# A conditioning matmul read in whole rows beside the first MLP, and an output projection that begins before the last DeltaNet head ends

## The chip, the cores and the metric

The kernel runs on one core of a Trainium2 chip. The metric is the device time of one launch in microseconds (us). Five engines matter: PE (TensorE, the matmuls; PEld is its weight load), DVE (VectorE), ACT (ScalarE), POOL (GpSimd) and SP (SyncE), whose queue here issues nearly all loads. Each engine, and each queue of transfers, works strictly in the order in which its instructions stand.

## The reference

One denoising step of a two-layer backbone over 640 tokens (128 context tokens and 512 latent tokens, width D = 1024). Layer 0 mixes tokens by softmax attention, layer 1 by gated DeltaNet with 8 heads; each layer ends in a squared-ReLU MLP of width 4096. Before each mixer and each MLP the activations are normalised and modulated by vectors that come from a conditioning vector:

```python
def modulation(cond, w_mod, b_mod):
    m = jax.nn.silu(cond) @ w_mod + b_mod
    return jnp.split(m[..., None, :], N_MOD, axis=-1)

def trunk_layer(x, mods, gain1, gain2, w1, w2, mixer):
    shift1, scale1, gate1, shift2, scale2, gate2 = mods
    mix, aux = mixer(rms_norm(x, gain1) * (1 + scale1) + shift1)
    x = x + gate1 * mix
    h = rms_norm(x, gain2) * (1 + scale2) + shift2
    x = x + gate2 * (jnp.square(jax.nn.relu(h @ w1)) @ w2)
    return x, aux
```

The DeltaNet mixer ends, for every head, in a gated norm, and then in the output projection over all heads:

```python
    o = rms_norm(o, norm_gain) * jax.nn.silu(z.reshape(B, T, DN_HEADS, DN_DV).astype(jnp.float32))
    out = o.reshape(B, T, DN_VAL).astype(h.dtype) @ w_out
```

## The kernel before, in words

Activations lie transposed: 8 tiles of 128 features by 640 tokens, handled in two halves of 320 tokens. A matrix product is made of column tiles of 128 output features. For one column tile and one half, each of 8 feature tiles takes three matmuls (`mm3`: high part by high part, high by low, low by high), 24 matmuls of 128x128 by 320 columns into one PSUM bank. Weights are loaded by SP into one of 3 `raw` buffers; ACT writes the high part and DVE (or POOL, where `eng` says so) the low part. The parts lie in `wpair` (6 buffers, 3 pairs; names `w`, `xin`, `y`) or in `wext` (10 buffers, names `wx`). `prefetch` fills `wpair` with the first three column tiles of the next product.

Python generators issue the program; a scheduler then sets the order on each engine and waits are added where a buffer or a value is not there yet. `pinned` runs the first MLP (128 steps of one column tile and half each) beside side work (`beside`), one side step for so many MLP steps. The side work is first the modulation of layer 1, slab 0: 1024 rows of `w_mod` by 2048 columns, as 8 feature rows k of four quarters q of 512 columns. Quarter q is a matmul with only 32 weight columns, put at column 32 q of the array; it writes rows 32 q to 32 q + 31 of one bank. A quarter in float32 shows as two MATMUL records. `modulate_pieces` loads a quarter (256 KB) into one of three `rawp` buffers and issues one quarter in each side step. After it `presplit` splits the DeltaNet's weights through `rawp` and `wpair` and writes them to DRAM.

In `delta` the heads pass through a pipeline of rounds (`weave` mixes the steps). `dn_out` ends a head: squares on ACT, a reciprocal root in small DVE operations, a multiply of the head's output (POOL for heads 0 to 6, DVE for head 7), five transposes on PE, the gate on DVE and a split into high and low. Heads 0 to 4 go to DRAM (`outd`) and are loaded and split again by `load_act` after the last round. Then the pool of `delta` closes, `mlp1` opens, `x` is loaded back (`reload`, from `xs`) and `dense` makes the output projection: three prefetched column tiles, then the other five as one group, whose low parts POOL makes. `residual` adds each half tile to `x` and, by `norm_acc`, its squares to a sum.

Of the kernel before, what the change touches and what calls it, by code (L numbers as in the profile page):

```python
# [8 lines left out]
F32 = mybir.dt.float32  # L9
# [6 lines left out]
P = 128  # L16
D = 1024
FT = D // P
# [3 lines left out]
HALF = T // 2  # L22
NBLK = T // P
HEADS = 8
# [9 lines left out]
HALVES = ((0, HALF), (HALF, T))  # L34
# [3 lines left out]
GROUP = 5  # L38
# [3 lines left out]
DIRECT = 5  # L42
# [35 lines left out]
def weave(*parts):  # L78
    live = [[0, n, i, g] for i, (g, n) in enumerate(parts)]
    while live:  # L80
        live.sort(key=lambda e: ((e[0] + 1) / e[1], e[2]))
        e = live[0]
        try:
            next(e[3])
            e[0] += 1
        except StopIteration:
            live.pop(0)
# [5 lines left out]
def pinned(tc, main, n, side, m):  # L93
    nc = tc.nc
    last = {}
    why = mybir.DependencyInfo(mybir.DependencyClass.NoSync, mybir.DependencyReason.DATA)
    traced = lambda i: nc.cur_bb.bb.instructions[i:]
    at = len(traced(0))
    done = step = 0
    for _ in main:  # L100
        step += 1
        for i in traced(at):
            if i.engine in PINNED:
                last[i.engine] = i.name
        at = len(traced(0))
        while done * n < step * m and next(side, True) is None:
            done += 1
            for i in traced(at):
                if i.engine in last:
                    tc.add_manual_dep(i, last[i.engine], why, reason="paced")  # L110
            at = len(traced(0))
    drain(side)


def drain(g):
    for _ in g:
        pass


class Model:  # L120
# [332 lines left out]
    def piece(self):  # L453
        return self.scr("rawp", 3, [P, FT // 2, P])

    def modulate_pieces(self, l, slab):
        ps = self.ps("mod", 1)[:, :512]

        def load(n):
            k, q = divmod(n, 4)  # L460
            r = self.piece().rearrange("p k c -> p (k c)")
            c = slab * 2048 + q * 512
            self.nc.sync.dma_start(out=r, in_=self.a["w_mod"][l, k * P : (k + 1) * P, c : c + 512])
            return r

        raws = [load(n) for n in range(2)]
        for n in range(4 * FT):
            k, q = divmod(n, 4)
            if n + 2 < 4 * FT:
                raws.append(load(n + 2))  # L470
            self.nc.tensor.matmul(  # L471
                ps[32 * q : 32 * q + 32, :], self.cond[:, k, :], raws.pop(0),
                start=k == 0, stop=k == FT - 1, tile_position=(0, 32 * q),
            )
            yield
        yield from self.modulation(l, slab, ps, lambda: self.ps("mod", 1))

    def fetch_slots(self, src):
        out = []
# [295 lines left out]
    def psum(self, name):  # L775
        return self.tc.tile_pool(name=name, bufs=1, space=bass.MemoryType.PSUM)
# [204 lines left out]
    @staticmethod  # L981
    def b3(t):
        return t.rearrange("p (b i) -> p b i", b=NBLK)
# [251 lines left out]
    def dn_out(self, hd):  # L1235
        nc = self.nc
        st, b3 = self.st[hd], self.b3
        o = st["o"]
        sso = self.small("sso", [P, NBLK], 2)
        self.squares(self.main("a"), o, sso)  # L1240
        self.ts(sso, sso, 1.0 / P, ALU.mult, P * EPS * EPS, ALU.add)
        self.stt(sso, st["ssc"][:, 1, :], P * EPS, sso, ALU.mult, ALU.add)
        sso = self.rsqrt(sso)
        eng = nc.gpsimd if hd < HEADS - 1 else nc.vector
        self.tt(b3(o), b3(o), sso.unsqueeze(2).to_broadcast([P, NBLK, P]), ALU.mult, eng)
        ps = self.ps("big", 2, 1024)
        for s in self.blocks():
            self.tr(ps[:, s], o[:, s])
        out = self.main("a")
        self.stt(out, ps[:, :T], self.dg, st["z"], ALU.mult, ALU.mult)  # L1250
        if hd < DIRECT:
            nc.gpsimd.dma_start(out=self.outd[hd], in_=out)
        else:
            self.split_act(hd, out)
        del self.st[hd]
        yield

    def delta(self, h, first):
        nc, a = self.nc, self.a
        self.st, self.acts = {}, {}  # L1260
        self.outd = self.dp.tile([HEADS, P, T], F32, tag="outd", bufs=1, name="outd")
        self.lev = self.scr("lev", 1, [P, P])
        nc.sync.dma_start(out=self.lev, in_=a["lev"])
        self.levcols = self.scr("levc", 1, [P, sum(P // b for b in LEVELS[1:])])
        nc.sync.dma_start(out=self.levcols, in_=a["levcols"])
        NP = 64 + NBLK * NB
        self.pn = self.scr("pn", 1, [NP, BASE * BASE])
        self.pt = self.scr("ptri", 1, [NP, BASE * BASE])
        nc.vector.memset(self.pn, 0.0)
        nc.vector.memset(self.pt, 0.0)  # L1270
        nc.vector.memset(self.pt[:, :: BASE + 1], 1.0)
        done = []

        def gated(zs):
            for i in zs:
                yield from self.dn_z(h, i)
                if i < HEADS - 1:
                    yield from self.dn_out(i)
                done.append(i)

        def mods():
            for slab in (1, 2):
                yield from self.modulate(1, slab, self.fetch_mixed, self.dense_ps, True)

        wm = mods()
        for r in range(HEADS + 3):
            parts = []
            if 0 <= r - 3 < HEADS:
                parts.append((self.dn_scan(r - 3), 14))
            if 0 <= r - 2 < HEADS:  # L1290
                parts.append((self.dn_inverse(r - 2), 10))
            if 0 <= r - 1 < HEADS:
                parts.append((self.dn_decay(r - 1), 20))
            zs = ZROUNDS.get(r, ())
            if zs:
                parts.append((gated(zs), 20 * len(zs)))
            if r < HEADS:
                parts.append((self.dn_dense(h, r, first if r == 0 else None), 54))
            if r >= HEADS:
                parts.append((islice(wm, MODS[r - HEADS]), MODS[r - HEADS]))  # L1300
            weave(*parts)
        drain(wm)
        self.first = self.prefetch(a["dn_w_out"][0], 0, [f * P for f in range(FT)])
        for i in range(DIRECT):
            self.load_act(i)
        drain(self.dn_out(HEADS - 1))

    def load_act(self, hd):
        f = self.main("x")
        self.nc.sync.dma_start(out=f, in_=self.outd[hd])  # L1310
        self.split_act(hd, f)

# [6 lines left out]
    def run(self):  # L1319
        tc, nc, a = self.tc, self.nc, self.a  # L1320
        pool = lambda name: tc.tile_pool(name=name, bufs=1)
        psum = self.psum
        FC = [f * P for f in range(FT)]
        with psum("ps0") as self.pq:
# [3 lines left out]
            x = []  # L1328
# [7 lines left out]
            h = self.first_norm(x, gm)  # L1336
        with pool("attn") as self.ph:
            self.attention(h, x)
            first = self.prefetch(a["attn_w_out"][0], 0, FC)
        with pool("mlp0") as self.ph, psum("ps3") as self.pq:  # L1340
            self.extra = 3
            x = self.reload(self.xd)
            h = self.new_h()
            nxt = []

            def mid():
                nxt[:] = self.prefetch(a["mlp_w1"][0], 0, FC)
                self.mod_norm(x, 0, 1, h, 0)

            weave((self.modulate(0, 2, self.fetch_raw), 18),  # L1350
                  (self.dense(a["attn_w_out"][0], 0, FC, self.att, self.residual(x, 0, 2), first=first, last=GROUP, mid=mid), 16))
            self.mod_norm(x, 0, 1, h, 1)
            h2 = self.new_h()
            nxt2 = []

            def mid2():
                w = a["dn_w_in"][0]
                nxt2[:] = [self.pair(w, 0, kind * D) for kind in (1, 0, 2)]
                self.mod_norm(x, 1, 0, h2, 0)

            def beside():
                yield from self.modulate_pieces(1, 0)
                yield from self.presplit()

            pinned(tc, self.mlp(0, h, x, nxt, mid2), 128, beside(), 98)
            self.mod_norm(x, 1, 0, h2, 1)
            h = h2
            xd = self.spill(x, nc.scalar)
        with pool("delta") as self.ph, psum("ps4") as self.pq:
            self.extra = 0  # L1370
            self.delta(h, nxt2)
        with pool("mlp1") as self.ph, psum("ps5") as self.pq:
            self.extra = 4
            acts = [self.acts[i] for i in range(HEADS)]
            x = self.reload(xd)
            h = self.new_h()
            nxt3 = []

# [1 line left out]
                nxt3[:] = self.prefetch(a["mlp_w1"][1], 0, FC)  # L1380
                self.mod_norm(x, 1, 1, h, 0)

            drain(self.dense(a["dn_w_out"][0], 0, FC, acts, self.residual(x, 1, 2), first=self.first, last=GROUP, mid=mid3, eng=nc.gpsimd))
            self.mod_norm(x, 1, 1, h, 1)
            fn = a["final_norm"]
            gain = self.wp.tile([P, D], F32, tag="wpair", bufs=self.NW, name="fgain")
# [73 lines left out]
```

## Time and profile before

| | us |
|---|---|
| median of 3 runs (lowest, highest) | 1906.38 (1905.86, 1908.35) |
| the profiled execution's own time | 1908.76 |
| its span, first to last instruction | 1906.9 |
| PE busy in it | 1816.6 (95%) |
| PEld, DVE busy | 1660.6, 990.3 |
| ACT, POOL busy | 754.5, 311.9 |
| granted TensorE clock, mean | 0.982 |

The span is one core's; 1.9 us of the profiled time lie outside it. A busy share is a mean over stages, so a stage is read by what its engines wait for there. A granted clock of 1.00 is 2.4 GHz, 0.50 is 1.2 GHz.

### The profile page before, as it was taken

To read this page: it belongs to the slowest core of one execution; us is meant where nothing else is said; L and a number is where in the kernel's file an instruction comes from. 1 tells how busy PE (TensorE), PEld (TensorE's weight loads), DVE (VectorE), ACT (ScalarE), POOL (GpSimd) and SP (SyncE) were. 2 spreads that over 40 slices of the span, in tenths; PEclk is the share of its full clock that TensorE was granted. 3 is DMA by queue.
4 is the path that set the end of the run, shared out by engine and by line. 5 is a ranking of instruction groups with operands and counts; after the bars stand their busy time and mean duration, and the time that the engine had idled before them with its cause. 6 is when DMAs were issued, how large, how long until landed. Compare 5 with 4: busy or idle time off the path is not lost.

```text
span 1906.9 us, 31083 instructions
## 1 busy us (share of the span) xinstructions
PE 1816.6 (95%) x11981; PEld 1660.6 (87%) x11981; DVE 990.3 (52%) x2293; ACT 754.5 (40%) x1725; POOL 311.9 (16%) x405
## 2 busy tenths in 40 slices
PE   6999999999999999999899999999899999999997
PEld 2778877888889999999889989776699999999997
DVE  4646662733244555555778877653655334343332
ACT  2445552421133443434756655623433223131331
POOL 2344221400001111142212111110241000000012
PEclk8899999999999999999999999999899999999999
DMA  7651137323347787843434324563712222222211
GB/s 278 219 157 43 34 109 212 103 76 113 102 127 254 227 269 225 257 160 128 129 111 118 81 86 131 167 189 135 224 53 79 70 75 78 78 74 70 78 45 56
DMA packets 291370, 248.84 MB, mean 130 GB/s; under 512 B 45104, under 2 KB 247239, under 8 KB 291223
## 3 DMA queue, kind: packets, MB, share of 16 engines
q1 hardware_dynamic: 271376, 207.85, 36.4%
q0 software_dynamic: 9136, 32.18, 4.6%
q10 hardware_dynamic: 10710, 6.83, 1.2%
q8 instruction: 94, 1.54, 0.3%
q14 instruction: 54, 0.43, 0.1%
HBM read 199.00 MB, written 45.20 MB: 128 GB/s over the span
## 4 chain that ended last, share of the span: by engine, by line
PE 75%; DVE 15%; DMA 5%; issue 2%; ACT 1%; POOL 1%; SPq 1%; POOLq 0%; ACTq 0%; DVEq 0%
PE dense L173 33%; PE pd L173 29%; PE scan L173 3%; PE big L173 2%; DVE cv L166 2%; DVE ptmp L160 2%; PE mod L471 2%; PE pd L408 1%; PE mod L408 1%; DVE ptri L1083 1%; PE big L176 1%; DVE wide L160 1%; DVE a L160 1%; DMA ptmp<-gmd 1%; PE S L173 1%
## 5 line engine op out<-in xcount | busy, mean ns | idle before, releaser
L173 PE MATMUL pd<-h,w 128*128 128x320 f32 x2016 | 353.6, 320 | 10.7 <-ACT cv L163 6.3
L173 PE MATMUL dense<-a,wx 128*128 128x320 f32 x2238 | 340.9, 311 | 2.4 <-ACT wx L163 1.8
L173 PEld LDWEIGHTS dense<-a,wx 128*128 128x128 f32 x2238 | 332.5, 189 | 11.2 <-issue 4.2
L173 PEld LDWEIGHTS pd<-h,w 128*128 128x128 f32 x2016 | 300.6, 189 | 38.3 <-issue 21.8
L163 ACT ACTIVATE wx<-raw 128x1024 fp32r<-128x1024 f32 x132 | 139.6, 1058 | 369.8 <-PE dense L173 234.0
L173 PEld LDWEIGHTS dense<-h,wx 128*128 128x128 f32 x1776 | 261.5, 188 | 9.2 <-issue 9.2
L173 PE MATMUL dense<-h,wx 128*128 128x320 f32 x1776 | 266.9, 309 | 0.0
L160 DVE TENSOR_TENSOR wx<-raw,wx 128x1024 fp32r<-128x1024 f32 x127 | 159.2, 1256 | 163.9 <-ACT wx L163 142.3
L173 PE MATMUL pd<-a,wx 128*128 128x320 f32 x1284 | 195.1, 310 | 0.0
L173 PEld LDWEIGHTS pd<-a,wx 128*128 128x128 f32 x1284 | 189.7, 188 | 4.2 <-issue 1.7
L166 DVE SCALAR_TENSOR_TENSOR x<-dense,c,x 128x320 f32<-128x320 f32 (+2 forms) x152 | 61.9, 435 | 191.6 <-PE dense L173 191.5
L173 PE MATMUL pd<-h,wx 128*128 128x320 f32 x1008 | 152.7, 309 | 0.0
L173 PEld LDWEIGHTS pd<-h,wx 128*128 128x128 f32 x1008 | 148.7, 188 | 4.2 <-issue 3.4
L160 POOL TENSOR_TENSOR x<-x,half 128x320 f32<-128x320 f32 x48 | 54.6, 1137 | 515.7 <-ACT half L163 508.4
L163 ACT ACTIVATE a<-half 128x320 fp32r<-128x320 f32 x128 | 59.9, 471 | 115.0 <-DVE half L166 115.0
L925 POOL DMA_DIRECT2D wd<-w x58 | 31.1, 536 | 398.9 <-ACT w L163 355.1
L160 DVE TENSOR_TENSOR a<-half,a 128x320 fp32r<-128x320 f32 x128 | 62.7, 492 | 64.1 <-ACT a L163 64.0
L166 DVE SCALAR_TENSOR_TENSOR x<-pd,c,x 128x192 f32<-128x192 f32 (+2 forms) x88 | 35.9, 436 | 102.5 <-PE pd L173 102.4
L166 DVE SCALAR_TENSOR_TENSOR cv<-cv,c,cv 128x644 f32<-128x644 f32 x84 | 78.2, 931 | 20.0 <-ACT cv L163 18.9
L163 ACT ACTIVATE half<-x 128x320 f32<-128x320 f32 x56 | 26.1, 467 | 106.2 <-DVE x L166 106.1
L173 PE MATMUL big<-wide,a 128*128 128x128 f32 x480 | 63.4, 278 | 1.0 <-DMA wide<-td 0.9
L173 PEld LDWEIGHTS big<-wide,a 128*128 128x128 f32 x480 | 58.0, 191 | 5.8 <-ACT a L163 1.7
(286 smaller groups left out, 2528.4 us busy)
## 6 DMA issues: line engine op xcount, KB each, us to landing
raw<-in_mlp_w SPq DMA_DIRECT2D x128, 512.0 KB
wd<-w POOLq DMA_DIRECT2D x58, 512.0 KB, 4.7
w<-wd SPq DMA_DIRECT2D x58, 512.0 KB
raw<-in_w_mod SPq DMA_DIRECT2D x48, 512.0 KB
rawp<-in_dn_w_in SPq DMA_DIRECT2D x58, 256.0 KB
a<-in_w_mod SPq DMA_DIRECT2D x48, 256.0 KB
rawp<-in_w_mod SPq DMA_DIRECT2D x32, 256.0 KB
raw<-in_attn_w_in SPq DMA_DIRECT2D x12, 512.0 KB
```

The source lines that it names most:

```text
L160: (eng or self.nc.vector).tensor_tensor(out=out, in0=in0, in1=in1, op=op)
L163: self.nc.scalar.activation(out=out, in_=in_, func=func, **kw)
L166: self.nc.vector.scalar_tensor_tensor(out=out, in0=in0, scalar=s, in1=in1, op0=op0, op1=op1)
L173: self.nc.tensor.matmul(out, l, r, start=first, stop=last)
L176: self.nc.tensor.transpose(out, in_, self.ident[:n, :n])
L408: nc.tensor.matmul(ps[32 * q : 32 * q + 32, :], self.cond[:, k, :], views[q], start=k == 0, stop=k == FT - 1, tile_position=(0, 32 * q),)
L471: self.nc.tensor.matmul(ps[32 * q : 32 * q + 32, :], self.cond[:, k, :], raws.pop(0), start=k == 0, stop=k == FT - 1, tile_position=(0, 32 ...
L925: self.nc.gpsimd.dma_start(out=d[z], in_=pair[z].bitcast(F32).rearrange("p k c -> p (k c)"))
L1083: nc.vector.tensor_reduce(out=t[:, BASE * i : BASE * i + i], in_=o, axis=AX.X, op=ALU.add)
```

## The change

There are two parts. First, the modulation beside the first MLP goes through `modulate`, which the kernel already uses elsewhere, with a new `fetch_pairs`: each feature row k comes as two loads of 512 KB into the `wpair` buffers, one row ahead, and a side step issues all four quarters of a row. The modulation takes 9 side steps instead of 33, and the pacing number goes from 98 to 74.

Second, the output projection's three prefetched tiles, in both halves, begin inside `delta` (`out_begin`): six half tiles in six PSUM banks (two `dense`, two `scan`, two halves of one `big`), first heads 0 to 6 for all six, then head 7 for all six, then the six residual sums. `x` is reloaded before it. The squares of these three tiles are summed after the pool has closed, and the group of five follows as before. `load_act` now stands in the last round, behind head 7's gate projection, and loads into `h` buffers; the multiply of head 6 moves from POOL to DVE.

```diff
+    def fetch_pairs(self, src):
+        out = []
+        for i in range(2):
+            r = self.wp.tile([P, 2, 512], F32, tag="wpair", bufs=self.NW, name=self.nm("wm"))
+            self.nc.sync.dma_start(out=r, in_=src[:, i * 1024 : (i + 1) * 1024].rearrange("p (q c) -> p q c", q=2))
+            out += [r[:, 0, :], r[:, 1, :]]
+        return out
...
-        eng = nc.gpsimd if hd < HEADS - 1 else nc.vector
+        eng = nc.gpsimd if hd < HEADS - 2 else nc.vector
...
+            if i == HEADS - 1:
+                for j in range(DIRECT):
+                    self.load_act(j)
+                    yield
...
-        for i in range(DIRECT):
-            self.load_act(i)
         drain(self.dn_out(HEADS - 1))
 
+    def out_begin(self, x):
+        wide = self.ps("big", 2, 1024)
+        banks = [self.dense_ps() for _ in range(2)] + [self.ps("scan", 2) for _ in range(2)] + [wide[:, :512], wide[:, 512:]]
+        todo = [(o, half, banks.pop(0)[:, :HALF]) for o in range(len(self.first)) for half in range(2)]
+        for ks in (range(HEADS - 1), (HEADS - 1,)):
+            for o, half, ps in todo:
+                lo, hi = HALVES[half]
+                for k in ks:
+                    w, act = self.first[o], self.acts[k]
+                    self.mm3(ps, (w[0][:, k, :], w[1][:, k, :]), (act[0][:, lo:hi], act[1][:, lo:hi]),
+                             k == 0, k == HEADS - 1)
+        sink = self.residual(x, 1, 2, False)
+        for t in todo:
+            sink(*t)
...
-                yield from self.modulate_pieces(1, 0)
+                yield from self.modulate(1, 0, self.fetch_pairs, early=True)
                 yield from self.presplit()
 
-            pinned(tc, self.mlp(0, h, x, nxt, mid2), 128, beside(), 98)
+            pinned(tc, self.mlp(0, h, x, nxt, mid2), 128, beside(), 74)
...
             self.delta(h, nxt2)
+            x = self.reload(xd)
+            self.out_begin(x)
...
+            for half in range(2):
+                for o in range(len(self.first)):
+                    self.norm_acc(x, o, half)
...
-            drain(self.dense(a["dn_w_out"][0], 0, FC, acts, self.residual(x, 1, 2), first=self.first, last=GROUP, mid=mid3, eng=nc.gpsimd))
+            done = len(self.first)
+            sink = self.residual(x, 1, 2)
+            drain(self.dense(a["dn_w_out"][0], 0, FC[done:], acts, lambda o, half, ps: sink(o + done, half, ps), last=GROUP, mid=mid3, eng=nc.gpsimd))
```

The order on PE early in the first MLP, before: between two half tiles (`pd`, `dense`; 24 matmuls each) stands one quarter of the modulation.

```order
L173 MATMUL pd_3893<-h_3010,w_3445 128x320
L471 MATMUL mod_3817<-rawp_3856,c_97 32x512
L173 MATMUL pd_3927<-h_2996,w_3450 128x320
...
L173 MATMUL dense_860_3958<-h_3010,w_3457 128x320
L471 MATMUL mod_3817<-rawp_3890,c_97 32x512
L173 MATMUL dense_867_3998<-h_2996,wx_3994 128x320
```

And of the change at the same place (`x2` is the two quarters of one load; `wm` lies in `wpair`):

```order
L173 MATMUL pd_3939<-h_3011,w_3450 128x320
L408 MATMUL mod_3817<-wm_3818,c_97 32x512 x2
L173 MATMUL pd_3939<-h_3010,w_3451 128x320
L173 MATMUL dense_862_3970<-h_2996,w_3456 128x320
...
L408 MATMUL mod_3817<-wm_3820,c_97 32x512 x2
...
L173 MATMUL pd_4091<-h_3010,wx_4088 128x320
L408 MATMUL mod_3817<-wm_4046,c_97 32x512 x2
L408 MATMUL mod_3817<-wm_4048,c_97 32x512 x2
L173 MATMUL pd_4130<-h_2996,wx_4087 128x320
```

The first quarter stands four half tiles later than before. In the first five rows k the two loads' quarters stand as two groups, 4 to 13 matmuls apart; in the last three rows all four stand together. That makes 13 groups instead of 32.

The order in SP's queue at the same place, before, where `raw` are the MLP's weights:

```order
L212 DMA raw_4483<-in_mlp_w 128x8x128
L463 DMA rawp_3856<-in_w_mod 128x512
L463 DMA rawp_3890<-in_w_mod 128x512
...
L463 DMA rawp_4134<-in_w_mod 128x512
L212 DMA raw_4545<-in_mlp_w 128x8x128
```

And of the change:

```order
L212 DMA raw_4529<-in_mlp_w 128x8x128
L460 DMA wm_3818<-in_w_mod 128x1024
L460 DMA wm_3820<-in_w_mod 128x1024
...
L460 DMA wm_4198<-in_w_mod 128x1024
L460 DMA wm_4200<-in_w_mod 128x1024
L212 DMA raw_4595<-in_mlp_w 128x8x128
```

All 16 loads of the modulation now stand in one run, behind the eleventh and ahead of the twelfth load of MLP weights; before, they alternated with them.

The order on PE at the end of `delta`, before; the transposes of head 7 are `big<-c,a`, and `x` are head 7's parts:

```order
L173 MATMUL pd_14526<-a_14171,w_14360 128x320
L176 MATMUL big_14415<-c_82,a_14007 128x128 x5
L173 MATMUL dense_2669_14467<-a_14365,w_14347 128x320
...
L173 MATMUL dense_2669_14467<-x_14423,w_14347 128x320
```

And of the change:

```order
L173 MATMUL scan_14415<-a_14294,w_14351 128x320
L176 MATMUL big_14383<-c_82,a_13975 128x128 x5
L173 MATMUL scan_14415<-a_14295,w_14351 128x320
...
L173 MATMUL big_14411<-a_14288,w_14357 128x320
...
L173 MATMUL pd_14412<-x_14391,w_14345 128x320
...
L173 MATMUL pd_14669<-a_14288,wx_14617 128x320
```

Ahead of head 7's transposes stand 67 matmuls of the projection instead of 42, and behind them 59 that do not need head 7 (17 of `scan`, 42 of `big`) instead of 21; then come the 18 of head 7.

## Rows read from the trace of the kernel before

**Rows 1.** The page: busy us by engine, and the chain that ended last.

```profile
PE 1816.6 (95%) x11981; PEld 1660.6 (87%) x11981; DVE 990.3 (52%) x2293; ACT 754.5 (40%) x1725; POOL 311.9 (16%) x405
PE 75%; DVE 15%; DMA 5%; issue 2%; ACT 1%; POOL 1%; SPq 1%; POOLq 0%; ACTq 0%; DVEq 0%
```

**Rows 2.** Windows of the first MLP: us, PE busy (records), clock, DMA, GB/s.

```profile
373.97:542.97 169.00, 169.00 (x974) 1.00 0.33 95
562.46:826.53 264.07, 264.07 (x1803) 1.00 0.80 248
```

**Rows 3.** Groups by line on PE, 373.97 to 542.97 us: the modulation's.

```profile
L471 PE MATMUL mod<-rawp,c 128*32 128x512 f32 x60 | 31.4, 604 | 0.0
```

**Rows 4.** Timeline of PE, modulation of layer 0: start, us, what, idle before.

```profile
286.33 1.05 PE L408 MATMUL mod<-raw,c 128*32 128x512 f32 x4 [1.19 <-DMA raw<-in_w_mod]
...
291.04 1.06 PE L408 MATMUL mod<-raw,c 128*32 128x512 f32 x8
292.04 3.77 PE L173 MATMUL dense<-a,w 128*128 128x320 f32 x24
...
305.74 1.71 PE L408 MATMUL mod<-raw,c 128*32 128x512 f32 x8
...
325.94 1.05 PE L408 MATMUL mod<-raw,c 128*32 128x512 f32 x4
326.93 1.15 PE L173 MATMUL dense<-a,wx 128*128 128x320 f32 x6
```

**Rows 5.** Timeline of SP's queue there: loads of 512 KB of `w_mod`.

```profile
279.63 0.81 SPq L439 DMA_DIRECT2D raw<-in_w_mod  x2
...
302.13 0.81 SPq L439 DMA_DIRECT2D raw<-in_w_mod  x2
```

**Rows 6.** Timeline of PE at the start of the first MLP.

```profile
362.05 0.58 PE L289 MATMUL nps<-c,x 128*128 128x1 f32 x2 [2.52 <-POOL x L160]
362.50 3.60 PE L173 MATMUL dense<-h,w 128*128 128x320 f32 x14
365.94 0.28 PE L289 MATMUL nps<-c,half 128*128 128x1 f32 x2
```

**Rows 7.** Windows of 2 us: PE busy (records), granted clock, DMA share, GB/s.

```profile
362.00:364.00 2.00, 1.95 (x8) 0.50 0.92 274
...
1374.00:1376.00 2.00, 1.17 (x5) 0.50 1.00 320
...
1378.00:1380.00 2.00, 2.00 (x12) 0.71 1.05 401
```

**Rows 8.** Timeline of PE from the end of the scan into the output projection.

```profile
1362.01 6.79 PE L173 MATMUL pd<-a,w 128*128 128x320 f32 x34 [1.31 <-DVE a L160]
1373.84 1.33 PE L176 MATMUL big<-c,a 128*128 128x128 f32 x5 [5.04 <-DVE a L160]
1376.15 4.69 PE L173 MATMUL dense<-a,w 128*128 128x320 f32 x21 [0.98 <-DVE a L166]
...
1392.12 0.60 PE L173 MATMUL dense<-x,w 128*128 128x320 f32 x3
1392.56 3.23 PE L173 MATMUL dense<-a,wx 128*128 128x320 f32 x21
```

**Rows 9.** Timeline of DVE: head 7's reciprocal root and multiply.

```profile
1364.68 0.17 DVE L160 TENSOR_TENSOR rst<-rsy 128x5 f32<-128x5 f32 x1
1364.89 2.41 DVE L166 SCALAR_TENSOR_TENSOR rst<-rst,sso 128x5 f32<-128x5 f32 x1
...
1372.96 0.82 DVE L160 TENSOR_TENSOR a<-a,rsy 128x640 f32<-128x640 f32 x1
```

**Rows 10.** Timeline of POOL: head 6's multiply and the low parts of weights.

```profile
1336.85 1.26 POOL L160 TENSOR_TENSOR a<-a,rsy 128x640 f32<-128x640 f32 x1 [18.85 <-DVE rsy L166]
...
1364.88 7.03 POOL L160 TENSOR_TENSOR wx<-raw,wx 128x1024 fp32r<-128x1024 f32 x3 [3.60 <-ACT wx L163]
```

**Rows 11.** Timeline of SP's queue: heads 0 to 4, and the reload of x.

```profile
1352.81 0.57 SPq L1310 DMA_DIRECT2D x<-outd  x1
...
1372.35 2.06 SPq L545 DMA_DIRECT2D x<-xs  x4
```

More of the change, by code (lines that the diff above doesn't have):

```diff
@@ L454, in piece @@
         return self.scr("rawp", 3, [P, FT // 2, P])
[L456 to L476, printed above, removed]
+    def fetch_pairs(self, src):
[5 more added lines that the diff above has]
+        return out
     def fetch_slots(self, src):
@@ L1303, in delta @@
         self.first = self.prefetch(a["dn_w_out"][0], 0, [f * P for f in range(FT)])
-        for i in range(DIRECT):
-            self.load_act(i)
         drain(self.dn_out(HEADS - 1))
+    def out_begin(self, x):
[12 more added lines that the diff above has]
+            sink(*t)
     def load_act(self, hd):
-        f = self.main("x")
+        f = self.main("h")
         self.nc.sync.dma_start(out=f, in_=self.outd[hd])
@@ L1374, in run @@
             acts = [self.acts[i] for i in range(HEADS)]
-            x = self.reload(xd)
+            for half in range(2):
+                for o in range(len(self.first)):
+                    self.norm_acc(x, o, half)
             h = self.new_h()
```

## The prediction

> **What bounds the kernel now.** I read the page first: PE is busy 95% of the span and three quarters of the chain that ended last is PE's [rows 1]. So a change pays only if it takes work off PE's queue, or fills a place where PE stands still. Both parts of the change aim at PE, one in each way, so I went to the two stages.
>
> In the first MLP PE never stands still while the modulation runs: the window from 373.97 to 542.97 is busy in full, 169.00 of 169.00 us, at a clock of 1.00, and so is the later window without modulation [rows 2]. What the modulation costs there is therefore PE time and nothing else. At the end of the DeltaNet stage it is the other way: PE stops for 1.31, then 5.04, then 0.98 us, each time for DVE [rows 8], and the clock is 0.50 just behind the long stop [rows 7].
>
> **Part one, the price of a quarter.** The window without modulation has 1803 matmuls in 264.07 us, 0.1465 us each [rows 2]. The window with it has 974 records, 60 of them the modulation's [rows 3], that is 30 quarters and 914 other matmuls. Those cost 914 x 0.1465 = 133.9 us; the other 35.1 us are the 30 quarters: 1.17 us each. All 32 cost 37.5 us.
>
> What does a group of quarters cost? The trace has both forms in the modulation of layer 0. Eight records, four quarters, began at 291.04 and the next matmul at 292.04: 1.00 us. Four records, two quarters, began at 325.94 and the next matmul at 326.93: 0.99 us [rows 4]. So neighbours in different quarters of the array run side by side, and a group of two or four takes what one takes. I price every group at the 1.17 us of a single one, since that includes what the matmuls beside it lose. The order shows 13 groups: 13 x 1.17 = 15.2 us. PE's work falls by 37.5 - 15.2 = **22.3 us**.
>
> **Part one, the new waits.** Before, the loads had buffers of their own. Now they wait for `wpair`, which at the start of the MLP holds the three prefetched tiles. A buffer is free after the tile's second half, so the distance from there to the group that needs the load is the cover. By the order it is 23 matmuls (3.4 us) for the first load, 17 matmuls and a group (2.5 + 1.2 = 3.7 us) for the third, and 8 matmuls (1.2 us) for the fifth. From the seventh load on a buffer comes from an earlier row of the modulation, freed a whole row before.
>
> How long does such a load take? Two were issued from 302.13 on, the second some 0.5 us later [rows 5]; the group of four at 305.74 spans 1.71 us where the one at 291.04 spans 1.06 [rows 4], so the second load was there 0.65 us into it, at about 306.4: 3.7 us. That is the short end. The long end: a load issued at 279.63 still held PE until 286.33 [rows 4, 5], 6.7 us, with others ahead of it. I take 3.7, since SP has been standing and little is ahead of the first ones. Then the waits are 0.3, 0, and 2.5 us; six loads are issued together behind the fifth buffer, so I add 0.7 for the sixth: 3.5 us in all. With 6.7 they are 3.3 + 3.0 + 5.5 + 1 = 12.8; with all of it hidden, 0.
>
> A wait of that size also costs clock: a stop of 2.52 us at 359.5 was followed by a clock of 0.50 [rows 6, 7], and the 14 matmuls behind it took from 362.50 to 365.94, 3.44 instead of 14 x 0.1465 = 2.05 us [rows 6]. That is 1.4 us; I count it once (bounds 0 and twice, 2.8). Part one is then 22.3 - 3.5 - 1.4 = **17.4 us** (bounds 6.7 and 22.3).
>
> What is queued behind SP's wait: the twelfth load of MLP weights and everything after it. The eleven ahead are issued by then, and the order has the twelfth used about 350 matmuls (51 us) behind the row that frees the last buffer, so I cost it at nothing; if that cover were gone, a load of 3.7 to 6.7 us would stand in front of PE once. The splits of the DeltaNet's weights start earlier and are spread wider, on ACT, DVE and POOL, where PE did not wait for them before: nothing.
>
> **Part two.** Until the transposes of head 7 PE has 67 matmuls instead of 42, and behind them 59 that need nothing of head 7. Before, the three tiles were through in both halves at 1392.56 [rows 8]. What sets the new end is when the transposes can run, and that is DVE's multiply, done at 1373.8 [rows 9]. Its chain is long for a reason that the rows show: small DVE operations of 0.17 us take 2.41 us, one for each of three splits that POOL runs from 1364.88 to 1371.91 [rows 9, 10], and there are three such, 3 x 2.24 = 6.7 us of the chain. The change leaves those splits on POOL, still five of them, and the squares of head 7 still stand between two of them on ACT, with three behind. So I keep 1373.8.
>
> From there: five transposes at half clock, 1.33 us [rows 8]; some 4 us more at half clock, as the rows before show up to about 1379 [rows 7], at 3.44 / 14 = 0.246 us a matmul, 16 matmuls; then 43 + 18 matmuls at 0.1465, 8.9 us. Sum 1373.8 + 1.33 + 4.0 + 8.9 = 1388.0: **4.5 us** earlier. If PE hardly stops before the transposes and the clock stays up, it is 1373.8 + 0.7 + 77 x 0.1465 = 1385.8, 6.8 us. If head 7's chain were free of POOL, the multiply would be done at 1367.1 and PE, not DVE, would be last there: 42 matmuls ended at 1368.8 before, 25 more are 3.7 us, 1372.5, or up to 4 us less if heads 0 to 4 come earlier (they stood at 1352.81 behind a load that now follows them [rows 11]). From 1368.5 on: 1368.5 + 0.7 + 11.3 = 1380.5, 12 us. The bad end stands among the rivals.
>
> Costed at nothing: the reload of `x` (issued at 1372.35 before [rows 11], behind loads whose buffers POOL frees; the first sum that needs it is at about 1386, so some 10 us cover it, and beyond that every us is on the path); the six late squares and four late sums, beside ten half tiles of 3.5 us; head 6's multiply, 1.26 us on POOL [rows 10] now on DVE, in a stretch in which PE had matmuls.
>
> **Sum.** 17.4 + 4.5 = 21.9 us. The profiled execution's 1908.8 would become 1886.9 (span 1885.0); the median of the runs is 2.4 below that execution, so 1906.4 becomes **1884.5**.
>
> **The rivals.**
> - *POOL crowds head 7.* If the projection's weights come a little earlier, all five splits on POOL can follow on one another under the chain of head 7 instead of three: two more times 2.3 us, the multiply at 1378.5, the tiles through at 1392.7, and part two gives nothing: 1906.4 - 17.4 + 0.1 = 1889.1. For it: SP now issues four of these loads where one stood ahead of the heads. Against it: the last three need the squares or buffers that POOL frees. The Trainium skill, "SBUF — State Buffer", section "Who interferes with whom", states the rule: a VectorE instruction with two SBUF inputs and a GpSimd instruction that reads SBUF exclude each other, and the later one blocks until the other has ended. By that rule part two would give as little as this rival says; the three stretched operations agree with it.
> - *Better on both sides.* Loads hidden (22.3) and head 7 free of POOL (12): 1872.1. Against it: 8 matmuls do not cover a load, and POOL's five splits have no other place.
> - *The quarters do not run side by side* when they stand among matmuls of the whole array: 32 x 1.17 us remain, and the new waits of 4.9 us eat part two: 1906.4 + 4.9 - 4.5 = 1906.8, no change. Against it: the two forms at 0.99 and 1.00 us had whole-array matmuls on both sides [rows 4].
> - *Slower: every row's loads are exposed.* All eight rows wait on PE for a load of 3.7 to 6.7 us, 30 to 54 us, because buffer, load and use follow one another with no row ahead: 1906.4 - 22.3 - 4.5 + 30 = 1909.6, up to 1933. It decides from 3.4 us a row on ((22.3 + 4.5) / 8). Against it: six buffers hold three rows, and in the order the last three rows stand 48 matmuls (7 us) apart.
>
> **How the numbers follow.** Forecast 0.62 (its own range 1879 to 1891: waits of 1 to 8 us, part two 2 to 8); POOL crowds 0.14; better on both sides 0.12; no side by side 0.04; slower 0.04; the rest 0.04, small gains. The range 1877 to 1893 leaves out the best of the better and the last three, about 2 in 10. A measurement of this kernel can tell a change of about 0.2% (3.8 us) from none. Faster by more than that: 0.62 + 0.14 + 0.12 + 0.04 = 0.92; within it 0.04; slower 0.04.
>
> **What would show it.** On PE in the first MLP: 13 groups of modulation near 1.0 us each, two or four quarters together; waits of 2 to 4 us at the fifth load and little elsewhere; the end of the MLP 15 to 20 us earlier. At the end of the DeltaNet stage: 67 matmuls, then a stop of some us that DVE's multiply ends, still with DVE operations of 2.3 us under POOL's splits, then a stream without a stop to the group of five, which starts 4 to 5 us earlier counted from the end of the scan. It is wrong if groups of four take over 2 us, if PE waits for loads in the fourth row or later, if weights of the MLP come late behind SP's wait, or if a residual sum waits for `x`.

## The result, and the profile after

The changed kernel takes 1882.64 us (median of 4 runs, 1880.47 to 1888.92) where the kernel before took 1906.12 (1905.41 to 1908.35) beside it: a ratio of 0.9874, with a 95% interval of 0.9848 to 0.9899. The forecast was 1884.5 us with a range of 1877 to 1893. The profiled execution went from 1908.76 to 1883.34 us, 25.4 us less, and its span from 1906.9 to 1881.5.

The page after, busy times and the chain that ended last, answers to [rows 1]:

```profile
PE 1793.3 (95%) x11981; PEld 1657.3 (88%) x11981; DVE 991.3 (53%) x2294; ACT 753.9 (40%) x1725; POOL 311.6 (17%) x404
PE 75%; DVE 14%; DMA 5%; issue 2%; ACT 2%; POOL 1%; SPq 1%; POOLq 0%; ACTq 0%; DVEq 0%
```

PE has the same 11981 records and is busy for 23.3 us less. DVE, ACT and POOL work as long as before. So most of the gain is PE work that no longer takes time, not waiting that is gone.

Where in the span? Two stages can be laid side by side. The first runs from the last matmul of the norm ahead of the first MLP to the first matmul of the norm behind it. As a window of that stretch (us, busy time with records for PE, PEld, DVE, ACT and POOL, then clock, DMA share and GB/s), first before, then after:

```profile
370.25:836.91 466.66, 466.66 (x2998) 434.62 (x2997) 210.36 (x350) 157.53 (x264) 46.62 (x74) 1.00 0.60 183
```

```profile
367.30:813.44 446.14, 445.02 (x2994) 431.38 (x2993) 209.33 (x350) 157.40 (x264) 45.91 (x74) 1.00 0.62 191
```

The stretch is 20.5 us shorter, the clock is 1.00 in both, and after it holds 1.12 us (446.14 - 445.02) in which PE stood. The two windows do not hold quite the same work: of the modulation the one before holds 62 records (31 quarters, the first stood ahead of it), the one after all 64, and the one before holds six more matmuls of the MLP, 0.9 us at 0.1465, which after stand ahead of the norm. The view of PE's waits in this stretch after (what waited, for what, us in total, times, longest) has one row for all of that:

```profile
PE mod L408 <- DMA wm<-in_w_mod: 1.1, 2, 0.6
```

PE's timeline there, after, which answers to [rows 4]; a quarter is two records:

```profile
381.11 1.05 PE L408 MATMUL mod<-wm,c 128*32 128x512 f32 x4 [0.48 <-DMA wm<-in_w_mod]
...
388.60 1.05 PE L408 MATMUL mod<-wm,c 128*32 128x512 f32 x4 [0.64 <-DMA wm<-in_w_mod]
...
391.39 1.05 PE L408 MATMUL mod<-wm,c 128*32 128x512 f32 x4
...
407.88 1.06 PE L408 MATMUL mod<-wm,c 128*32 128x512 f32 x8
408.87 3.80 PE L173 MATMUL pd<-h,wx 128*128 128x320 f32 x24
```

And a single quarter in the first MLP before:

```profile
373.97 1.04 PE L471 MATMUL mod<-rawp,c 128*32 128x512 f32 x2
374.95 3.79 PE L173 MATMUL dense<-h,w 128*128 128x320 f32 x24
```

Groups of two and of four quarters span 1.05 and 1.06 us, the single quarter 1.04, and the group of four gives PE back 0.99 us after its start (407.88 to 408.87), the single one after 0.98. The third row after is the fifth load's group: it waits for nothing. SP's timeline has that load issued long ahead of it:

```profile
382.58 0.43 SPq L460 DMA_DIRECT2D wm<-in_w_mod  x1
```

The second stage is the end of the DeltaNet. I count it from the last row `scan<-blk,wide` on PE (1354.79 before, 1331.72 after) to the first matmul behind head 7's part of the three tiles (1392.56 before, in [rows 8]; 1365.72 after): 37.77 us before, 34.00 after. PE's timeline after, where [rows 8] is that of before:

```profile
1331.72 0.39 PE L173 MATMUL scan<-blk,wide 128*128 128x128 f32 x2
...
1342.56 2.35 PE L173 MATMUL scan<-a,w 128*128 128x320 f32 x15
1351.83 1.33 PE L176 MATMUL big<-c,a 128*128 128x128 f32 x5 [6.92 <-DVE a L160]
1352.81 4.31 PE L173 MATMUL scan<-a,w 128*128 128x320 f32 x17
1356.96 6.29 PE L173 MATMUL big<-a,w 128*128 128x320 f32 x42
1363.08 1.04 PE L173 MATMUL pd<-x,w 128*128 128x320 f32 x6
...
1365.72 1.93 PE L173 MATMUL pd<-a,wx 128*128 128x320 f32 x12
```

The stop ahead of the transposes is still there and is longer, 6.92 us instead of 5.04, although 25 more matmuls stand ahead of it. Behind it PE runs through, first at half clock (windows of 2 us, as in [rows 7]):

```profile
1352.00:1354.00 2.00, 2.00 (x9) 2.00 (x10) 0.81 (x1) 0.00 (x0) 0.00 (x0) 0.50 1.09 364
1354.00:1356.00 2.00, 2.00 (x9) 2.00 (x9) 0.90 (x2) 0.74 (x1) 0.00 (x0) 0.50 1.03 384
1356.00:1358.00 2.00, 2.00 (x15) 2.00 (x14) 0.00 (x0) 0.00 (x0) 0.00 (x0) 0.92 1.04 402
```

What holds the transposes is the chain on DVE, and its timeline after, beside [rows 9], shows why it is long:

```profile
1339.99 2.37 DVE L170 TENSOR_SCALAR sso<-sso 128x5 f32<-128x5 f32 x1
1342.39 2.32 DVE L166 SCALAR_TENSOR_TENSOR sso<-ssc,sso 128x5 f32<-128x5 f32 x1
1344.74 2.27 DVE L170 TENSOR_SCALAR rsy<-sso 128x5 int32<-128x5 int32 x1
...
1347.45 2.26 DVE L166 SCALAR_TENSOR_TENSOR rsy<-rst,rsy 128x5 f32<-128x5 f32 x1
...
1350.94 0.83 DVE L160 TENSOR_TENSOR a<-a,rsy 128x640 f32<-128x640 f32 x1
```

And POOL's, beside [rows 10]:

```profile
1336.31 10.68 POOL L160 TENSOR_TENSOR wx<-raw,wx 128x1024 fp32r<-128x1024 f32 x4 [42.01 <-ACT wx L163]
1347.35 2.34 POOL L160 TENSOR_TENSOR wx<-raw,wx 128x1024 fp32r<-128x1024 f32 x1 [0.36 <-ACT wx L163]
```

All five splits now follow on one another from 1336.31 on. Four operations of the chain take 2.3 us for 0.17, one under each of the last four splits; before it was three. Each of the four ends 0.02 or 0.03 us behind its split, the last at 1349.71 behind 1349.69. The first split holds an operation ahead of the chain.

### The profile page after: what moved, and what is told of

It is laid out like the page before. It is cut to its first block, busy times and chain, and to the rows that moved or that the text cites. A ratio compares the mean times of both kernels' runs of the same rounds, so it can differ in the third digit from the quotient of the medians.

```text
span 1881.5 us, 31040 instructions
## 1 busy us (share of the span) xinstructions
PE 1793.3 (95%) x11981; PEld 1657.3 (88%) x11981; DVE 991.3 (53%) x2294; ACT 753.9 (40%) x1725; POOL 311.6 (17%) x404
## 4 chain that ended last, share of the span: by engine, by line
PE 75%; DVE 14%; DMA 5%; issue 2%; ACT 2%; POOL 1%; SPq 1%; POOLq 0%; ACTq 0%; DVEq 0%
PE dense L173 32%; PE pd L173 29%; PE scan L173 3%; PE big L173 2%; DVE cv L166 2%; PE mod L408 2%; DVE ptmp L160 2%; PE pd L408 2%; PE big L176 1%; DVE ptri L1069 1%; DVE a L160 1%; DMA raw<-in_w_mod 1%; DVE wide L160 1%; DMA ptmp<-gmd 1%; PE S L173 1%
## 5 line engine op out<-in xcount | busy, mean ns | idle before, releaser
L166 DVE SCALAR_TENSOR_TENSOR x<-dense,c,x 128x192 f32<-128x192 f32 (+2 forms) x147 | 59.6, 433 | 175.3 <-PE dense L173 175.3
L166 DVE SCALAR_TENSOR_TENSOR x<-pd,c,x 128x128 f32<-128x128 f32 (+2 forms) x87 | 35.8, 439 | 105.5 <-PE pd L173 105.4
```

The source lines that it names most:

```text
L166: self.nc.vector.scalar_tensor_tensor(out=out, in0=in0, scalar=s, in1=in1, op0=op0, op1=op1)
```

## The experiments

Besides the times, one table of the two stages. "MLP" is the window above, "transposes" and "tiles" are their starts counted from the last row `scan<-blk,wide`, each in the profiled execution. The expectations count "tiles" from that row's second matmul to the end of the last one, which gives 0.2 us more.

| kernel | median us | ratio (95%) | MLP | transposes | tiles |
|---|---|---|---|---|---|
| before | 1906.12 | 1 | 466.66 | 19.05 | 37.77 |
| the change | 1882.64 | 0.9874 (0.9848, 0.9899) | 446.14 | 20.11 | 34.00 |
| rows alone | 1886.06 | 0.9887 (0.9868, 0.9906) | 446.52 | 19.08 | 39.13 |
| projection alone | 1904.02 | 0.9987 (0.9972, 1.0001) | 466.66 | 20.05 | 33.63 |
| quarters apart | 1904.31 | 0.9986 (0.9971, 1.0001) | 465.13 | 20.13 | 33.80 |
| low parts on DVE | 1869.60 | 0.9807 (0.9785, 0.9829) | 446.04 | 14.21 | 23.76 |
| fours | 1876.33 | 0.9813 (0.9795, 0.9832) | 439.08 | 20.02 | 33.58 |
| fours, low parts on DVE | 1865.28 | 0.9748 (0.9725, 0.9770) | 439.07 | 14.15 | 23.68 |
| rows, low parts on DVE | 1881.93 | 0.9846 (0.9826, 0.9866) | 445.88 | 15.18 | 34.32 |
| heads loaded late | 1885.97, one run | | 445.18 | 19.98 | 33.58 |

The kernel before beside the experiments had medians of 1906.83 (rows alone to low parts on DVE) and 1911.44 (the rest), with runs from 1901 to 1915. Ratios go by that neighbour; across the two groups of experiments 0.2% between ratios means little, and the stages decide. A single profiled execution decides even less by its whole time: the last matmul of the norm ahead of the first MLP ends between 360.84 us (rows alone) and 373.07 us (fours, low parts on DVE) in these ten, though PE's order up to there is the same in all of them.

**Rows alone, projection alone.** Each part of the change without the other. In the first, the early matmuls, the earlier `load_act`, and head 6's multiply on DVE are taken back; in the second, the modulation:

```diff
 rows alone
-            x = self.reload(xd)
-            self.out_begin(x)
...
 projection alone
-                yield from self.modulate(1, 0, self.fetch_pairs, early=True)
+                yield from self.modulate_pieces(1, 0)
...
-            pinned(tc, self.mlp(0, h, x, nxt, mid2), 128, beside(), 74)
+            pinned(tc, self.mlp(0, h, x, nxt, mid2), 128, beside(), 98)
```

Expected of rows alone:

> Part one alone, the rest as before. My theory (side by side quarters, 13 groups for 32, waits near 1 us in all): about 20.5 us faster than before (1885 to 1887), the end of the first MLP some 20 us earlier counted from its first half tile, and everything behind it unchanged in length. Rival (the gain of the whole change comes mostly from the output projection): under 12 us. Rival (the two parts share a gain, through the clock or the loads): parts one and two alone do not add up to the whole within 3 us.

Expected of projection alone:

> Part two alone, with the modulation in single quarters as before. My theory: 3 to 5 us faster than before, the first three tiles through 3.5 to 5 us earlier counted from the end of the scan, with five splits of POOL in a row under the chain of head 7. Rival (POOL's five splits cost all that the early matmuls give): within 1.5 us of before. Rival (the early matmuls give more, and the rest was lost elsewhere): over 7 us faster.

The rows alone give 1.13% of 1906.83, 21.5 us (17.9 to 25.2 by the interval; the medians differ by 20.8), nearly all of the change. Their MLP is 20.1 us shorter than before. The end of their DeltaNet is the program of before, and yet the tiles come at 39.13 instead of 37.77: the transposes stand at 19.08 and 19.05, but behind them the clock stayed at 0.50 up to 1353 us, 8.2 us from the transposes' start at 1344.78, where before it was 0.71 from 4.2 us on [rows 7]. So 1.4 us between two entries of the last column can be the clock alone. The projection alone gives 0.13%, 2.5 us, with an interval from 5.3 faster to 0.2 slower: from the time it cannot be told whether it is the 3.8 us of its stage or nothing. Its stage, though, is 4.1 us shorter than before (33.63 against 37.77), and PE's timeline shows the same stop as in the change:

```profile
1367.38 1.32 PE L176 MATMUL big<-c,a 128*128 128x128 f32 x5 [6.87 <-DVE a L160]
```

**Quarters apart.** The whole change with the same loads, but one quarter in each side step, at the old pacing, so that 30 groups stand on PE instead of 13.

```diff
             for q in range(4):
...
+                if apart and q < 3:
+                    yield
...
-            pinned(tc, self.mlp(0, h, x, nxt, mid2), 128, beside(), 74)
+            pinned(tc, self.mlp(0, h, x, nxt, mid2), 128, beside(), 98)
```

> The whole change, but one quarter in each side step, with the same loads of whole rows. My theory: what gains is that neighbouring quarters run side by side, so with 30 groups for 13 PE has 17 x 1.17 = 19.9 us more, and the time goes back to 1900 to 1904. Rival (what gains is the larger loads or the other buffers): no more than 5 us slower than the whole change.

It falls back to 1904.31. The window of its MLP:

```profile
366.60:831.73 465.13, 464.65 (x2993) 433.56 (x2992) 210.20 (x350) 157.60 (x264) 46.55 (x74) 1.00 0.59 183
```

The loads, their size and their buffers are those of the change, and PE's work is again within 2.0 us of before; the time is 0.3 us above what was expected. So the larger loads give nothing by themselves; that the quarters stand together gives it. 17 groups more cost 464.65 - 445.02 = 19.6 us, 1.15 us each (the first row's quarters still stand in two pairs, the other 28 alone).

**Fours.** If groups are the price, fewer groups must pay. Issued in the order 2, 3, 0, 1, all four quarters of a row stand together.

```diff
-            for q in range(4):
+            for q in order:
...
-                yield from self.modulate(1, 0, self.fetch_pairs, early=True)
+                yield from self.modulate(1, 0, self.fetch_pairs, early=True, order=(2, 3, 0, 1))
```

> The whole change with one thing different: the quarters of a feature row are issued in the order 2, 3, 0, 1, so that all four of a row stand together behind the later of its two loads. 8 groups of modulation on PE instead of 13. Theory (a group costs one quarter, however many run side by side): 5 groups of 1.17 us less, 5.9 us, minus up to 1.5 us of new waits, since the first group now waits for both loads: 3 to 6 us faster than the change (which was at 0.9874 of the kernel before), so about 1877 to 1880 us, ratio near 0.985. In the trace: 8 groups of 8 records of about 1.05 us, none of 4 records. Rival (the waits for the second load eat what the groups give): PE stops of 3 us and more for loads, the time within 2 us of the change.

```profile
381.28 1.06 PE L408 MATMUL mod<-wm,c 128*32 128x512 f32 x8
384.96 1.06 PE L408 MATMUL mod<-wm,c 128*32 128x512 f32 x8
```

```profile
366.33:805.41 439.08, 439.07 (x2993) 430.65 (x2992) 209.08 (x350) 157.39 (x264) 45.87 (x74) 1.00 0.63 194
```

There are 8 groups of 8 records (two are shown), and PE waits for no load at all (439.07 busy of 439.08): the first group stands 11 matmuls later than in the change, which covers what the change waited for. The stretch is 7.06 us shorter: 1.12 of waits and 5.95 for 5 groups, 1.19 each. The time, 1876.33, is 6.3 below the change, 0.7 below the range that was expected; the ratio is better than that, by a neighbour that ran slower. The rival, waits that eat the gain, did not happen.

**Low parts on DVE.** The whole change with POOL's splits of the projection's weights given back to DVE:

```diff
-            drain(self.dense(a["dn_w_out"][0], 0, FC[done:], acts, lambda o, half, ps: sink(o + done, half, ps), last=GROUP, mid=mid3, eng=nc.gpsimd))
+            drain(self.dense(a["dn_w_out"][0], 0, FC[done:], acts, lambda o, half, ps: sink(o + done, half, ps), last=GROUP, mid=mid3))
```

> The whole change, with the low parts of the projection's group of five on DVE in place of POOL. My theory (POOL's five splits stretch the chain of head 7, four small operations and one split at 2.3 to 2.8 us each): the small operations fall to 0.17 us, four splits of 1.25 us stand among them instead, head 7's multiply ends 4 to 6 us earlier counted from the end of the scan, the stop before the transposes shrinks from 6.9 to 1 to 3 us, and the kernel is 3 to 6 us faster than the whole change (1877 to 1880). Rival (the chain is bound by the loads or by ACT): the multiply ends less than 1.5 us earlier and the time stays within 2 us.

It is 13 us below the change by the medians, more than twice the upper end of that, and 10.2 us by the stage. On DVE and PE:

```profile
1340.03 0.16 DVE L170 TENSOR_SCALAR sso<-sso 128x5 f32<-128x5 f32 x1
...
1344.83 0.83 DVE L160 TENSOR_TENSOR a<-a,rsy 128x640 f32<-128x640 f32 x1
```

```profile
1341.70 3.83 PE L173 MATMUL scan<-a,w 128*128 128x320 f32 x25
1345.71 0.77 PE L176 MATMUL big<-c,a 128*128 128x128 f32 x5 [0.18 <-DVE a L160]
1346.23 0.39 PE L173 MATMUL scan<-a,w 128*128 128x320 f32 x1
1346.46 6.32 PE L173 MATMUL big<-a,w 128*128 128x320 f32 x42
```

The chain's operations are back at 0.16 and 0.17 us, though DVE makes the five splits itself (1.2 us each; two of them stand in the chain, where four were expected), and the transposes come 5.9 us earlier, as expected. What I had not priced came behind: the schedule now puts 16 more matmuls ahead of the transposes, 1 instead of 17 of `scan` stands behind them, and they just fill the wait, so that the stop is 0.18 us. The clock stays at 1.00 (from 1342 to 1354 us); the 42 matmuls take 6.32 us from the start on. From the transposes to the tiles it is 9.55 us (1345.71 to 1355.26) instead of 13.89: 4.3 us, of which the 16 matmuls are 2.3 (at 0.1465) and the rest is clock.

**Rows, low parts on DVE.** The rows alone, without the early projection, with low parts on DVE (both edits shown above).

> Part one of the change alone (no early output projection), with the low parts of the projection's weights on DVE. It tells apart what the 13 us of the fourth experiment need. Theory A (both are needed: a chain free of POOL, and the early matmuls that keep PE busy until the chain is done): head 7's multiply ends 4 to 6 us earlier counted from the end of the scan, but PE runs out of its 42 matmuls ahead of the transposes and still stops for 1 to 4 us, and the clock falls to 0.50 behind it; three tiles through 30 to 34 us after the scan's last wide step, where the change has 34.2 and the fourth experiment 23.9; ratio 0.984 to 0.987 (part one alone: 0.9887). Theory B (it is all POOL's splits): no stop and full clock here too, tiles through at 27 us or less after the scan, ratio 0.983 or lower.

```profile
1346.83 0.76 PE L176 MATMUL big<-c,a 128*128 128x128 f32 x5 [1.68 <-DVE a L160]
1349.52 4.72 PE L173 MATMUL dense<-a,w 128*128 128x320 f32 x21 [1.93 <-DVE a L166]
```

```profile
1350.00:1352.00 2.00, 2.00 (x9) 2.00 (x9) 0.82 (x1) 0.24 (x1) 0.00 (x0) 0.50 0.91 248
```

Theory A holds: the transposes come 3.9 us earlier than in rows alone, but PE runs out of work twice, for 1.68 and 1.93 us, the clock falls to 0.50, and the tiles come at 34.32 (34.5 as the expectation counts, half a us beyond it). Against rows alone (39.13) the free chain gives 4.8 us of the stage, the early matmuls give 5.1 (the change), and both together 15.4; counted from before (37.77) it is 3.5, 3.8 and 14.0. With the free chain alone PE lacks matmuls, with the early matmuls alone it waits for the chain.

**Fours, low parts on DVE.** Both edits on the whole change.

> The whole change with both edits: all four quarters of a row together, and the low parts of the output projection's weights made by DVE instead of POOL. If the two gains lie in different stages and add, the ratio is that of the low parts on DVE alone (0.9807) less 0.002 to 0.003: about 0.978, 1864 to 1867 us. If they do not add, it stays at 0.981, about 1870 us.

1865.28 us, ratio 0.9748: the fastest of all, 17 us below the change. The stages are those of the two single edits, 439.07 and 23.68, so they add.

**Heads loaded late.** The whole change, but `load_act` back behind the last round.

```diff
-            if i == HEADS - 1:
-                for j in range(DIRECT):
-                    self.load_act(j)
-                    yield
...
+        for i in range(DIRECT):
+            self.load_act(i)
```

> The whole change, but with heads 0 to 4 loaded and split where they were before, after the last round, still into the h buffers. Theory (DVE's multiply of head 7 sets when the transposes run, and the loads of the heads are early enough either way): the three tiles are through 33 to 36 us after the scan's last wide step (34.2 in the change), less than 1.5 us apart in that stage. Rival (the early loads are what lets 67 matmuls stand ahead of the transposes): PE waits for the parts of heads 0 to 4, the tiles come 4 us later or more, at 38 us or over.

```profile
1354.79 1.33 PE L176 MATMUL big<-c,a 128*128 128x128 f32 x5 [6.93 <-DVE a L160]
```

The stage is 33.58 us, 0.4 from the change, with the same stop for the same multiply: the early loads are not what part two needs.

## Why the prediction was right, step by step

- **The bound.** PE was the engine to relieve in the first MLP: 21.6 us less busy time there shortened the stretch by 20.5.
- **The price of a group, 1.17 us.** Right. The change's 13 groups against 31 in the window of before give (466.66 - 0.9 - 445.02) / 18 = 1.15, where 0.9 is the six matmuls that the window of before holds besides; quarters apart gave 1.15, fours 1.19. For 19 groups less PE's work fell by about 21.9 us, where 22.3 was predicted.
- **The new waits, 3.5 us, and 1.4 us of clock.** This is the term that was mis-sized: 1.1 us and nothing. The duration of a load was not the error. The first was issued at 377.14 and landed when its group began, at 381.11, 4.0 us; the fourth took from 382.20 to 388.60, 6.4 us; both lie within the bounds 3.7 and 6.7. The cover was the error. I had the fifth load wait for the last prefetched tile, 8 matmuls ahead of its group. It was issued at 382.58, right behind the fourth load (382.20): the first load's group had ended by then (381.11 + 1.05 = 382.16), so that its buffer came free before the tile's, and the load had 8.8 us until 391.39. The ninth, issued at 390.18 when that tile was done, had 10.5 us until its group at 400.68. The clock stayed at 1.00 through both waits. So part one is 20.6 us instead of 17.4, inside the bounds given (6.7 to 22.3): the window's 20.5, and 1.0 for the quarter ahead of it (368.61 to 369.59), less 0.9 for the six matmuls.
- **Nothing behind SP's wait.** Right: the only wait of PE in the stretch is the one shown, and no weights of the MLP came late.
- **Part two, 4.5 us.** The stage gives 3.8. From the transposes on the sum was right: 14.2 us predicted from 1373.8 to 1388.0, 13.9 measured from 1351.83 to 1365.72. The step that was off is "so I keep 1373.8": the transposes come 1.06 us later, counted from the scan. The rival of five splits in a row happened on POOL, but its price did not: one split more fell into the chain, not two. The chain lasts 11.8 us from `sso` (1339.99) to the end of the multiply instead of 9.7 (from 1364.09 before), 2.1 more, and it begins 1.0 earlier. Low parts on DVE shows that the splits are the cause, and that the time was there to be had, 10 us of it: "better on both sides" priced a chain free of POOL at 12 us, and from before to low parts on DVE the stage is 14.0 shorter, by an edit that the change does not make.
- **Nothing for `x`, the late sums and head 6.** From the transposes on PE has no stop up to the group of five, so neither `x` nor the sums hold it. Head 6's multiply on DVE was not tried by itself.
- **The sum.** 20.6 + 3.8 = 24.4 us against 25.4 in the profiled pair; the medians give 23.5 against the forecast of 21.9. That the forecast is only 1.6 off by the medians is partly luck: part one gave 3.2 us more than forecast and part two 0.7 less. What lies outside the two stages moved too. Ahead of the first window the change's profiled execution is 2.95 us earlier (367.30 against 370.25), of which the moved quarter and matmuls explain 0.1; between the stages it takes 0.40 us longer, and behind them 1.44 longer, where the clock behind a stop that the change does not touch (below) differs. A term of 2 us can't be read from whole times here, only from its stage.

## What to carry to other kernels

Matmuls of 32 weight columns in different quarters of the array cost by group here, not by piece (1.15 to 1.19 us a group of one, two or four): put all that can run side by side next to one another in PE's queue, even if the first must wait for a later load. When POOL helps with large operations while DVE walks a chain of tiny ones that PE waits for, count each POOL operation as one link of that chain (2.3 us for 0.17 here); a stop of PE needs both a short chain and enough matmuls ahead of it to go away, and either alone gave a quarter to a third of what both gave (3.5 or 3.8 of 14.0 us from before). When you count the cover of a load, follow the buffer that it is given, not the one that comes free last.

## What was not expected of the hardware

- A `TENSOR_SCALAR` with a single input in SBUF, of 128x5, took 2.37 and 2.27 us under POOL's splits and 0.16 us without them; I had thought of operations with two inputs. The Trainium skill, "SBUF — State Buffer", section "Who interferes with whom", says that `tensor_scalar` too can enter a mode that uses both ports and then contends with GpSimd, when its operands meet certain conditions. The trace agrees in that both ended 0.03 us behind POOL's split (1342.36 behind 1342.33, 1347.02 behind 1346.99); which mode they ran in no row shows.
- A split takes POOL 2.3 to 3.1 us (7.03 for three before, 10.68 for four after) where DVE makes one in 1.2, so POOL's help held DVE longer than DVE's own work would have.
- Loads of 512 KB issued close together moved 326 GB/s over 8 us of the first MLP, and PE stood for 0.60 us of it:

```profile
388.00:396.00 8.00, 7.40 (x40) 4.31 (x42) 0.98 (x2) 0.91 (x2) 0.00 (x0) 1.00 0.94 326
```

In the norm behind the output projection PE stops for 2.5 us (2.49 us ahead of 1432.75 before, 2.48 ahead of 1405.92 after, 2.44 in rows alone), and what follows differs by profile. Windows of 10 us from the end of that stop, rows alone, before, and the change:

```profile
1404.98:1414.98 10.00, 9.67 (x67) 9.32 (x68) 7.17 (x20) 2.99 (x6) 1.28 (x2) 1.00 0.55 163
```

```profile
1432.75:1442.75 10.00, 10.00 (x61) 9.90 (x62) 6.17 (x18) 2.39 (x4) 0.43 (x1) 0.83 0.54 159
```

```profile
1405.92:1415.92 10.00, 10.00 (x51) 10.00 (x52) 4.70 (x15) 1.45 (x2) 0.00 (x0) 0.66 0.54 158
```

The same stop is followed by no half clock, some of it, and much of it, and PE gets through 67, 61 and 51 records. From the tiles to the end of the span these three take 513.3, 514.3 and 515.8 us, and fours, with a clock of 0.56 in the 10 us behind its stop, 517.3. What sets how long the clock stays low was not tried.
